# A hybrid decoder layer on one core: the MLP's first product with activations stationary, its result turned by VectorE and transfers

## The chip, the cores and the metric

The kernel runs on one core of one Trainium2 chip. Its time is the device time of one execution in microseconds (us); three executions of the kernel before took 1132.5, 1133.02 and 1133.17 us (median 1133.02). The engines are named as the profile names them: PE is TensorE's matmul, PEld its weight load, DVE is VectorE, ACT is ScalarE, POOL is GpSimd, SP is the engine that issues nearly all DMAs.

## The reference, cut to what matters

One layer on 256 tokens of width 2048, all in float32: RMSNorm, one input projection, two kinds of attention, an output projection added to the residual, then RMSNorm, an MLP and a last RMSNorm. The change is in the MLP:

```python
h = rmsnorm(x, ln2[l])                                       # 256 x 2048
x = x + jnp.square(jax.nn.relu(h @ w_mlp_in[l])) @ w_mlp_out[l]   # 2048 -> 8192 -> 2048
return rmsnorm(x, ln_f)
```

## The kernel before

**Precision.** Every float32 operand of a product is split in two parts that the matmul takes, a high one (rounded) and a low one (the rest), and a product is three passes: high x high, high x low, low x high.

**Weights.** All weights come in chunks of 1 MB (512 rows by 512 columns, on 128 partitions 4 x 512 numbers), loaded by SP into a ring of buffers (three before the MLP, six in it). A chunk is two jobs. For each job ACT writes the high part `wh` (L214) and DVE the low part `wl` (L217), each 128 x 1024. The splits lie in `spool`, four buffers of each, and in the MLP every third job's (job number modulo 3 is 2) in a late pool `mlp["split"]`, two of each (L210, L874). In the MLP a split is written five jobs before its products. When a chunk's second job is split, its buffer is given to the load of a later chunk.

**The MLP** goes through the 8192 inner columns in four quarters. A quarter is four groups of `in_group` (512 inner columns each, 8 jobs) and then four groups of `out_group` (512 output columns each, 8 jobs). `in_group` uses `products_T` (L264): the weights are stationary, and the activations move. For each 128 inner columns and each 128 rows of weights there are two matmuls: `wh` against both parts of the activations side by side, 512 moving columns (L271), and `wl` against the high part, 256 moving columns (L276). A job has 8 of each. The result stands with inner columns on partitions, which is how `out_group` needs it as its stationary operand. `out_group` uses `products_acc` (L248): activations stationary, 512 columns of weights moving, three matmuls (L258, L259, L260) for each 128 rows of weights and each 128 tokens, 12 in a job.

**After an `in_group`**, `evacuate` runs for each of its four 128-column blocks as the block's last matmul ends: ACT copies one half of the bank (L712), DVE adds the other (L714), takes relu and square in one instruction (L715), ACT rounds to the high part (L716), DVE makes the low part (L717). The results are the eight pairs `aT` of the quarter. Each `out_group` reads them in order, so the last `in_group`'s two pairs are needed from its seventh and eighth job on.

**Order.** Program order is the order in which the Python code runs: at job i the splits up to job i + 5 are asked for, then come the products, then what stands in `after`, then up to two steps of waiting side tasks (`tick`). A planner then orders each engine's instructions by a simulated timeline; on the chip every engine takes its own in that order. Accumulators of the MLP go round seven banks of PSUM.

**Where things lie.** Pools stand one behind another in each partition: `cpool`, `wpool`, `spool` (tiles of 4096 bytes), `apool` (16 tiles of 4096 bytes, all activations), `tiny` (21 tags of four buffers), and in the MLP `mlp_sb` (before: three `t1` and three `s` of 1024 bytes, and `lnf` of 8192, 14,336 bytes in all), `mlp_w` (three of 8192 bytes) and `mlp_split`.

Of the kernel before, what the change touches and what calls it, by code (L numbers as in the profile page):

```python
# [10 lines left out]
F32 = mybir.dt.float32  # L11
F32R = mybir.dt.float32r
BF16 = mybir.dt.bfloat16
AF = mybir.ActivationFunctionType
ALU = mybir.AluOpType
# [3 lines left out]
P = 128  # L19
S = 256  # L20
D = 2048
DFF = 4 * D
NT = S // P
KT = D // P
NB = 512
CK = 4
HK = 2
# [17 lines left out]
def tile_hybrid_layer(  # L45
# [21 lines left out]
    nc = tc.nc  # L67
# [5 lines left out]
    apool = ctx.enter_context(tc.tile_pool(name="apool", bufs=16))  # L73
# [91 lines left out]
    def add_chunk(view, products, after=None, pools=None):  # L165
        c = len(chunks)
        chunks.append(view)
        nh = CK // HK
        for h in range(nh):
            jobs.append((c, h, products, after if h == nh - 1 else None, pools))  # L170
# [3 lines left out]
    mlp = {"n": 0}  # L174
# [48 lines left out]
    side = deque()  # L223
    hooks = {}

    def tick(n=2):
        for task in list(side)[:n]:
            try:
                next(task)
            except StopIteration:  # L230
                side.remove(task)
# [16 lines left out]
    def products_acc(get_acc, act, k0, first, last):  # L248
        def f(h, wh, wl):
            acc = get_acc()  # L250
            for j in range(HK):
                kt = k0 + h * HK + j
                a = act(kt)
                for t in range(NT):
                    st = slice(t * P, (t + 1) * P)
                    s0 = first and h == 0 and j == 0
                    s1 = last and h == CK // HK - 1 and j == HK - 1
                    nc.tensor.matmul(acc[t], a[:, 0, st], wh[:, j, :], start=s0, stop=False)  # L258
                    nc.tensor.matmul(acc[t], a[:, 0, st], wl[:, j, :], start=False, stop=False)  # L259
                    state["mm"] = nc.tensor.matmul(acc[t], a[:, 1, st], wh[:, j, :], start=False, stop=s1)  # L260
        return f


    def products_T(get_acc, act, k0, done):  # L264
        def f(h, wh, wl):
            acc = get_acc()
            last = k0 + (h + 1) * HK == KT

            def high(i, j):
                kt = k0 + h * HK + j  # L270
                nc.tensor.matmul(acc[i], wh[:, j, i * P:(i + 1) * P], act(kt).rearrange("p a s -> p (a s)"),  # L271
                                 start=kt == 0, stop=False, skip_group_check=True)

            def low(i, j):
                kt = k0 + h * HK + j
                state["mm"] = nc.tensor.matmul(acc[i][:, S:2 * S], wl[:, j, i * P:(i + 1) * P], act(kt)[:, 0, :],  # L276
                                               start=False, stop=kt == KT - 1, skip_group_check=True)


            tiles = range(NB // P)  # L280
            for part in ([(i,) for i in tiles] if last else [tiles]):
                for one in (high, low):
                    for i in part:
                        for j in range(HK):
                            one(i, j)
                if last:
                    done(part[0])
        return f
# [393 lines left out]
    def bank(name):  # L682
        i = mlp["n"] % 7
        mlp["n"] += 1
        pool = mlp["ps"] if i < 3 else ps_acc
        return pool.tile([P, NB], F32, tag="acc", name=name)
# [3 lines left out]
    aT = {}  # L690
    ss3 = cpool.tile([P, NT, 5], F32, name="ss3")
    rs2 = {}

    def in_group(q, g):
        f0 = (q * FG + g) * NB
        acc = {}

        def get_acc():
            if not acc:
                for i in range(NB // P):  # L700
                    acc[i] = bank(f"ia{q}{g}{i}")
            return acc

        def evacuate(i):
            nm = f"{q}{g}{i}"
            kt = g * 4 + i
            if i % 2 == 0:
                pair = apool.tile([P, HK, 2, S], F32R, tag="act", name=f"aT{nm}")
                aT[q, kt // 2] = pair
            pair = aT[q, kt // 2]  # L710
            t1 = mlp["sb"].tile([P, S], F32, tag="t1", name=f"t1_{nm}")
            nc.scalar.copy(t1, acc[i][:, S:2 * S])  # L712
            s = mlp["sb"].tile([P, S], F32, tag="s", name=f"s_{nm}")
            nc.vector.tensor_tensor(s, acc[i][:, 0:S], t1, op=ALU.add)  # L714
            nc.vector.scalar_tensor_tensor(s, s, 0.0, s, op0=ALU.max, op1=ALU.mult)  # L715
            nc.scalar.copy(pair[:, i % 2, 0, :], s)  # L716
            nc.vector.tensor_tensor(pair[:, i % 2, 1, :], s, pair[:, i % 2, 0, :].bitcast(F32),  # L717
                                    op=ALU.subtract)

        for c in range(KT // CK):  # L720
            view = w_mlp_in[0, c * CK * P:(c + 1) * CK * P, f0:f0 + NB].rearrange("(k p) n -> p k n", p=P)
            add_chunk(view, products_T(get_acc, act_xs2, c * CK, evacuate))

    def out_group(q, nb):
        acc = {}

        def get_acc():
            if not acc:
                for t in range(NT):
                    acc[t] = bank(f"ma{q}{nb}{t}")  # L730
            return acc

        def act(kt):
            return aT[q, kt // 2][:, kt % 2]

        def after():
            for t in range(NT):
                residual(nb, t, acc[t], slice(0, NB))
                if q == FQ - 1:
                    square_sum(nb, t, slice(0, NB), nb)  # L740
                    nc.vector.tensor_tensor(xt[nb][:, t, :], xt[nb][:, t, :],
                                            lnf_t[:, nb * NB:(nb + 1) * NB], op=ALU.mult)

        r0 = q * (DFF // FQ)
        views = [w_mlp_out[0, r0 + c * CK * P:r0 + (c + 1) * CK * P,
                           nb * NB:(nb + 1) * NB].rearrange("(k p) n -> p k n", p=P)
                 for c in range(KT // CK)]
        if (q, nb) != (FQ - 1, 3):
            for c in range(KT // CK):
                add_chunk(views[c], products_acc(get_acc, act, c * CK, c == 0, c == KT // CK - 1),  # L750
                          after if c == KT // CK - 1 else None)
            return


        kept = {}
        half = NB // 2

        def passes(o, t, cs, kt, w):
            a = act(kt)
            wh, wl = w  # L760
            st = slice(t * P, (t + 1) * P)
            j = kt % HK
            nc.tensor.matmul(o, a[:, 0, st], wh[:, j, cs], start=kt == 0, stop=False)
            nc.tensor.matmul(o, a[:, 0, st], wl[:, j, cs], start=False, stop=False)
            nc.tensor.matmul(o, a[:, 1, st], wh[:, j, cs], start=False, stop=kt == KT - 1)

        def first_token_tile(c):
            def f(h, wh, wl):
                kept[c * (CK // HK) + h] = (wh, wl)
                for j in range(HK):  # L770
                    passes(get_acc()[0], 0, slice(0, NB), c * CK + h * HK + j, (wh, wl))
            return f

        def first_done():
            residual(nb, 0, acc[0], slice(0, NB))
            base = square_base(0, nb)
            square_sum(nb, 0, slice(0, NB), nb)
            finish_tokens(0, base)

        def second_token_tile(hc):  # L780
            def f(h, wh, wl):
                o = acc[1] if hc == 0 else bank("ma_last")
                cs = slice(hc * half, (hc + 1) * half)
                for kt in range(KT):
                    passes(o[:, :half], 1, cs, kt, kept[kt // HK])
                residual(nb, 1, o[:, :half], cs)
                if hc == 1:
                    base = square_base(1, nb + 1)
                square_sum(nb, 1, cs, nb + hc)
                if hc == 1:  # L790
                    finish_tokens(1, base)
            return f

        act_tag = (apool, "act")
        for c in range(KT // CK):
            add_chunk(views[c], first_token_tile(c), first_done if c == KT // CK - 1 else None,
                      (act_tag, act_tag) if c < 2 else None)
        for hc in range(2):
            jobs.append((None, 0, second_token_tile(hc), None, None))
# [71 lines left out]
    lnf_t = mlp["sb"].tile([P, D], F32, tag="lnf", name="lnf_t", bufs=1)  # L871
    nc.sync.dma_start(lnf_t, ln_f.partition_broadcast(P))
    mlp["w"] = ctx.enter_context(tc.tile_pool(name="mlp_w", bufs=W_BUFS))
    mlp["split"] = ctx.enter_context(tc.tile_pool(name="mlp_split", bufs=2))  # L874
    for _ in range(W_BUFS):
        issue_dma()
# [49 lines left out]
```

## Time and profile before

| | us |
|---|---|
| median of three executions | 1133.02 |
| the profiled execution's own time | 1131.97 |
| its span | 1130.3 |
| PE busy | 1119.3 (99%) |
| DVE busy | 662.8 (59%) |
| ACT busy | 536.8 (47%) |

The span runs from the first to the last instruction of the profiled execution; 1.67 us of its time lie around it. A matmul's busy time overlaps with its neighbours', since matmuls are pipelined: PE's pace is read from starts, or from the length of a stretch and its count of matmuls. The chain that ended last is PE for 99% of the span. The granted clock of PE is 1.00 of full speed in all stages of the MLP.

### The profile page before, as it was taken

What the parts mean: (1) busy time and instruction counts of PE and PEld (TensorE: products, weight loads), DVE (VectorE), ACT (ScalarE), POOL (GpSimd) and SP (SyncE); (2) the same over time, 40 slices, a digit from 0 to 9 for tenths busy, and PEclk for the clock granted to TensorE, in tenths of its full rate; (3) what the DMA queues carried; (4) which work ended last, traced back from release to release, by engine and by line L of the source; (5) the groups of instructions that cost most, each with busy time, mean ns of one, the idle gap of its engine ahead of it and who ended that gap; (6) DMA issues with size and microseconds to landing.
All of it is one profiled execution on the core that took longest, in us unless ns stands there. A gap on an engine that the chain in (4) does not pass through costs nothing.

```text
span 1130.3 us, 14306 instructions
## 1 busy us (share of the span) xinstructions
PE 1119.3 (99%) x5725; PEld 945.4 (84%) x5725; DVE 662.8 (59%) x929; ACT 536.8 (47%) x761; POOL 2.9 (0%) x16
## 2 busy tenths in 40 slices
PE   9999999999999999999999999999999999999996
PEld 6887888888888888888888888888888888888886
DVE  5756657756556565664455565455655544665752
ACT  5644545555555554543334444334544334454531
POOL 1000000000000000000000000000000000000000
PEclk9999999999999999999999999999999999999999
DMA  8745453555456855555556555555555556555502
GB/s 288 233 158 169 164 186 113 183 165 166 157 177 244 286 186 186 186 187 186 191 192 202 193 189 183 192 186 186 188 190 182 194 195 205 188 186 187 192 32 75
DMA packets 105207, 207.68 MB, mean 184 GB/s; under 512 B 4114, under 2 KB 5172, under 8 KB 105012
## 3 DMA queue, kind: packets, MB, share of 16 engines
q1 hardware_dynamic: 104852, 206.24, 55.0%
q8 instruction: 45, 0.74, 0.3%
q10 hardware_dynamic: 288, 0.52, 0.1%
q14 instruction: 22, 0.18, 0.0%
HBM read 204.65 MB, written 2.10 MB: 183 GB/s over the span
## 4 chain that ended last, share of the span: by engine, by line
PE 99%; DMA 0%; DVE 0%; SPq 0%; ACT 0%; issue 0%; DVEq 0%; ACTq 0%
PE ia L271 21%; PE ia L276 11%; PE ma L260 10%; PE ma L259 10%; PE ma L258 10%; PE acc_sk L271 3%; PE acc_sq L271 3%; PE oacc L260 3%; PE oacc L258 3%; PE oacc L259 3%; PE acc_dq L258 1%; PE acc_sq L276 1%; PE acc_sk L276 1%; PE acc_dk L258 1%; PE acc_dk L260 1%; PE acc_dq L260 1%
## 5 line engine op out<-in xcount | busy, mean ns | idle before, releaser
L217 DVE TENSOR_TENSOR wl<-w,wh 128x1024 fp32r<-128x1024 f32 (+1 forms) x385 | 469.6, 1222 | 383.7 <-ACT wh L214 382.3
L214 ACT CAST wh<-w 128x1024 fp32r<-128x1024 f32 (+1 forms) x385 | 402.0, 1047 | 465.7 <-PE ma L260 189.3
L271 PE MATMUL ia<-xs,wh 128*128 128x512 f32 x1024 | 267.7, 393 | 0.0
L271 PEld LDWEIGHTS ia<-xs,wh 128*128 128x128 f32 x1024 | 180.0, 189 | 28.4
L260 PE MATMUL ma<-wh,aT 128*128 128x512 f32 x480 | 187.9, 391 | 0.0
L259 PE MATMUL ma<-wl,aT 128*128 128x512 f32 x480 | 187.8, 391 | 0.0
L258 PE MATMUL ma<-wh,aT 128*128 128x512 f32 x480 | 187.7, 391 | 0.0
L276 PEld LDWEIGHTS ia<-xs,wl 128*128 128x128 f32 x1024 | 147.8, 189 | 15.8
L276 PE MATMUL ia<-xs,wl 128*128 128x256 f32 x1024 | 152.2, 282 | 0.0
L260 PEld LDWEIGHTS ma<-wh,aT 128*128 128x128 f32 x480 | 90.1, 188 | 19.8
L259 PEld LDWEIGHTS ma<-wl,aT 128*128 128x128 f32 x480 | 90.1, 188 | 19.8
L258 PEld LDWEIGHTS ma<-wh,aT 128*128 128x128 f32 x480 | 90.1, 188 | 19.7
L258 PE MATMUL oacc<-wh,mixT 128*128 128x512 f32 x128 | 50.6, 395 | 0.0
L259 PE MATMUL oacc<-wl,mixT 128*128 128x512 f32 x128 | 50.2, 392 | 0.0
L260 PE MATMUL oacc<-wh,mixT 128*128 128x512 f32 x128 | 49.9, 394 | 0.0
L271 PE MATMUL acc_sk<-xs,wh 128*128 128x512 f32 x128 | 36.7, 399 | 0.0
L271 PE MATMUL acc_sq<-xs,wh 128*128 128x512 f32 x128 | 34.9, 397 | 0.0
L712 ACT COPY t<-ia 128x256 f32<-128x256 f32 x64 | 23.8, 372 | 20.0 <-PE ia L276 20.0
L260 PEld LDWEIGHTS oacc<-wh,mixT 128*128 128x128 f32 x128 | 24.0, 188 | 5.0
L258 PEld LDWEIGHTS oacc<-wh,mixT 128*128 128x128 f32 x128 | 24.1, 188 | 4.9
L259 PEld LDWEIGHTS oacc<-wl,mixT 128*128 128x128 f32 x128 | 24.1, 188 | 4.9
L714 DVE TENSOR_TENSOR s<-ia,t 128x256 f32<-128x256 f32 x64 | 26.9, 420 | 1.9
(223 smaller groups left out, 1099.1 us busy)
## 6 DMA issues: line engine op xcount, KB each, us to landing
w<-in_w_mlp_in_dram SPq DMA_DIRECT2D x64, 1024.0 KB, 5.5
w<-in_w_mlp_out_dram SPq DMA_DIRECT2D x64, 1024.0 KB, 5.1
w<-in_w_in_dram SPq DMA_DIRECT2D x46, 1024.0 KB, 5.2
w<-in_w_out_dram SPq DMA_DIRECT2D x16, 1024.0 KB, 5.1
w<-in_w_in_dram SPq DMA_DIRECT2D x4, 512.0 KB, 7.9
x<-in_x_dram SPq DMA_DIRECT2D x3, 512.0 KB, 10.5
lnf_t<-in_ln_f_dram SPq DMA_DIRECT2D x1, 1024.0 KB, 6.4
out_dram<-x SPq DMA_DIRECT2D x4, 256.0 KB, 3.0
```

What stands on the lines that cost most here:

```text
L214: state["wh"] = nc.scalar.copy(wh[:, j], w[:, j])
L217: state["wl"] = nc.vector.tensor_tensor(wl[:, j], w[:, j], wh[:, j].bitcast(F32), op=ALU.subtract)
L258: nc.tensor.matmul(acc[t], a[:, 0, st], wh[:, j, :], start=s0, stop=False)
L259: nc.tensor.matmul(acc[t], a[:, 0, st], wl[:, j, :], start=False, stop=False)
L260: state["mm"] = nc.tensor.matmul(acc[t], a[:, 1, st], wh[:, j, :], start=False, stop=s1)
L271: nc.tensor.matmul(acc[i], wh[:, j, i * P:(i + 1) * P], act(kt).rearrange("p a s -> p (a s)"), start=kt == 0, stop=False, skip_group_check ...
L276: state["mm"] = nc.tensor.matmul(acc[i][:, S:2 * S], wl[:, j, i * P:(i + 1) * P], act(kt)[:, 0, :], start=False, stop=kt == KT - 1, skip_g ...
L712: nc.scalar.copy(t1, acc[i][:, S:2 * S])
L714: nc.vector.tensor_tensor(s, acc[i][:, 0:S], t1, op=ALU.add)
```

## The change

`in_group` now uses `products_acc` as `out_group` does: activations stationary, weights moving, two accumulators of 128 tokens x 512 inner columns. Its result has tokens on partitions. A side task turns it: DVE transposes blocks of 32 x 32 out of PSUM into `bl`, 16 DMAs issued by SP move the blocks between partitions into `hT`, DVE takes relu and square of `hT` in one instruction of 128 x 1024, and ACT and DVE write two pairs `aT` of 128 x 512 per part. `mlp_sb` then holds `hT` and `bl` (4096 bytes each) and `lnf`, 16,384 bytes. A tile of 352 numbers (1408 bytes) is put ahead of `mlp_split`.

```diff
+        def turn_task():
+            hT = mlp["sb"].tile([P, NT * 4, 4, 32], F32, tag="hT", name=f"hT{q}{g}", bufs=1)
+            bl = mlp["sb"].tile([P, NT, 4, 4 * 32], F32, tag="bl", name=f"bl{q}{g}", bufs=1)
+            for t in range(NT):
+                nc.vector.transpose(bl[:, t].rearrange("p f (k b) -> p f k b", b=32),
+                                    acc[t].rearrange("p (k f a) -> p f k a", k=4, f=4))
+            hv = hT.rearrange("p (t i) k b -> p t i (k b)", t=NT)
+            for i in range(4):
+                for f in range(4):
+                    nc.sync.dma_start(hv[f * 32:(f + 1) * 32, :, i, :], bl[i * 32:(i + 1) * 32, :, f, :])
+            yield
+            nc.vector.scalar_tensor_tensor(hT, hT, 0.0, hT, op0=ALU.max, op1=ALU.mult)
+            for kk in range(2):
+                pair = apool.tile([P, HK, 2, S], F32R, tag="act", name=f"aT{q}{g}{kk}")
+                s = hT[:, :, kk * 2:kk * 2 + 2, :].rearrange("p i k b -> p k i b")
+                hi = pair[:, :, 0, :].rearrange("p k (i b) -> p k i b", b=32)
+                lo = pair[:, :, 1, :].rearrange("p k (i b) -> p k i b", b=32)
+                nc.scalar.copy(hi, s)
+                nc.vector.tensor_tensor(lo, s, hi.bitcast(F32), op=ALU.subtract)
+                aT[q, g * 2 + kk] = pair
+                yield
+
+        def after():
+            side.append(turn_task())
+            tick(1)
...
-            add_chunk(view, products_T(get_acc, act_xs2, c * CK, evacuate))
+            add_chunk(view, products_acc(get_acc, act_xs2, c * CK, c == 0, c == KT // CK - 1),
+                      after if c == KT // CK - 1 else None)
...
         def act(kt):
+            while (q, kt // 2) not in aT:
+                tick()
             return aT[q, kt // 2][:, kt % 2]
...
     mlp["w"] = ctx.enter_context(tc.tile_pool(name="mlp_w", bufs=W_BUFS))
+    gap = ctx.enter_context(tc.tile_pool(name="mlp_gap", bufs=1))
+    gap.tile([P, 352], F32, name="mlp_gap")
     mlp["split"] = ctx.enter_context(tc.tile_pool(name="mlp_split", bufs=2))
```

## Rows read from the trace of the kernel before

**Rows 1.** The page: busy time, and the chain that ended last

```profile
PE 1119.3 (99%) x5725; PEld 945.4 (84%) x5725; DVE 662.8 (59%) x929; ACT 536.8 (47%) x761; POOL 2.9 (0%) x16
...
PE 99%; DMA 0%; DVE 0%; SPq 0%; ACT 0%; issue 0%; DVEq 0%; ACTq 0%
```

**Rows 2.** Windows of MLP stages, in_groups and out_groups in turn

```profile
core 0: us, PE busy (x) PEld busy (x) DVE busy (x) ACT busy (x) POOL busy (x), PEclk, DMA share, GB/s
410.00:500.38 90.38, 90.38 (x521) 79.21 (x520) 55.91 (x81) 45.25 (x68) 0.00 (x0) 1.00 0.59 191
500.38:588.37 87.99, 87.99 (x386) 72.09 (x385) 46.52 (x48) 35.15 (x37) 0.00 (x0) 1.00 0.56 187
588.37:677.92 89.55, 89.55 (x514) 78.56 (x512) 53.84 (x74) 42.58 (x60) 0.00 (x0) 1.00 0.58 193
677.92:765.92 88.00, 88.00 (x387) 72.10 (x385) 46.53 (x48) 35.13 (x37) 0.00 (x0) 1.00 0.57 187
765.92:855.45 89.53, 89.53 (x513) 78.56 (x512) 53.89 (x74) 42.58 (x60) 0.00 (x0) 1.00 0.58 193
855.45:943.39 87.94, 87.94 (x386) 72.09 (x385) 46.47 (x48) 35.14 (x37) 0.00 (x0) 1.00 0.57 186
943.39:1033.01 89.62, 89.62 (x514) 78.57 (x512) 53.90 (x74) 42.57 (x60) 0.00 (x0) 1.00 0.59 193
```

**Rows 3.** PE timeline: first matmuls of five successive out_group jobs (start, length)

```profile
500.38 0.40 PE L258 MATMUL ma<-wh,aT 128*128 128x512 f32 x1
...
503.11 0.40 PE L258 MATMUL ma<-wh,aT 128*128 128x512 f32 x1
...
505.90 0.39 PE L258 MATMUL ma<-wh,aT 128*128 128x512 f32 x1
...
508.64 0.39 PE L258 MATMUL ma<-wh,aT 128*128 128x512 f32 x1
...
511.36 0.40 PE L258 MATMUL ma<-wh,aT 128*128 128x512 f32 x1
```

**Rows 4.** Groups by form (count | busy us, mean ns | idle us): DVE, ACT

```profile
L217 DVE TENSOR_TENSOR wl<-w,wh 128x1024 fp32r<-128x1024 f32 x383 | 468.3, 1225 | 383.7 <-ACT wh L214 382.3
L714 DVE TENSOR_TENSOR s<-ia,t 128x256 f32<-128x256 f32 x64 | 26.9, 420 | 1.9
L428 DVE COPY T_dk<-tp_dk 128x512 f32<-128x512 f32 x4 | 2.8, 692 | 1.4 <-PE tp_dk L425 1.4
L847 DVE TENSOR_SCALAR x<-x,rf 128x512 f32<-128x512 f32 x2 | 1.0, 482 | 0.0
L716 ACT CAST aT<-s 128x256 fp32r<-128x256 f32 x64 | 24.2, 404 | 0.5
L156 ACT ACTIVATE mixT<-mtp_d,ghd 128x512 fp32r<-128x512 f32 x4 | 2.8, 688 | 3.7 <-PE mtp_d L446 3.7
```

**Rows 5.** SP timeline: four stores in a row; then the stores' time to landing

```profile
1113.74 1.88 SPq L848 DMA_DIRECT2D out_dram<-x  x4
...
DMA to landing us min/median/max: 1.9/2.5/3.0
```

**Rows 6.** SP timeline: weight loads about the second in_group's end, and that end on PE

```profile
455.33 0.40 PE L276 MATMUL ia<-xs,wl 128*128 128x256 f32 x2
...
451.62 0.37 SPq L195 DMA_DIRECT2D w<-in_w_mlp_in_dram  x1
457.87 0.37 SPq L195 DMA_DIRECT2D w<-in_w_mlp_out_dram  x1
...
w<-in_w_mlp_in_dram SPq DMA_DIRECT2D x64, 1024.0 KB, 5.5
```

**Rows 7.** Waits: who waited for whom, total us, times, longest

```profile
ACT wh L214 <- PE ma L260: 189.3, 116, 4.5
...
SPq L195 <- DVE wl L217: 772.3, 151, 13.3
```

**Rows 8.** DVE timeline after the first in_group: a split among the evacuation's instructions

```profile
433.88 0.43 DVE L715 SCALAR_TENSOR_TENSOR s<-s 128x256 f32<-128x256 f32 x1
434.26 1.23 DVE L217 TENSOR_TENSOR wl<-w,wh 128x1024 fp32r<-128x1024 f32 x1
435.40 1.09 DVE L717 TENSOR_TENSOR aT<-s,aT 128x256 fp32r<-128x256 f32 x3
```

**Rows 9.** SP timeline: small loads at the kernel's start, behind large ones

```profile
9.58 0.32 SPq L87 DMA_DIRECT2D rows<-in_diff_head_norm_dram  x1
...
18.45 0.33 SPq L91 DMA_DIRECT2D lamv<-in_lambda_k_dram  x1
```

More of the change, by code (lines that the diff above doesn't have):

```diff
@@ L699, in get_acc @@
             if not acc:
-                for i in range(NB // P):
-                    acc[i] = bank(f"ia{q}{g}{i}")
-            return acc
[L704 to L718, printed above, removed]
+                for t in range(NT):
+                    acc[t] = bank(f"ia{q}{g}{t}")
@@ new lines, in get_acc @@
+            return acc
+        def turn_task():
+            hT = mlp["sb"].tile([P, NT * 4, 4, 32], F32, tag="hT", name=f"hT{q}{g}", bufs=1)
+            bl = mlp["sb"].tile([P, NT, 4, 4 * 32], F32, tag="bl", name=f"bl{q}{g}", bufs=1)
+            for t in range(NT):
+                nc.vector.transpose(bl[:, t].rearrange("p f (k b) -> p f k b", b=32),
[15 more added lines that the diff above has]
+                yield
```

## The prediction, made before the change was run

> **What bounds the kernel now.** I read the page's busy times and its chain of waits first: PE is busy for 99% of the span and holds 99% of the chain that ended last [rows 1]. So only what changes PE's pace, or makes PE wait, can change the time. The windows by stage come next, because the page's mean hides the pace: in every MLP stage PE is busy for the whole window at a granted clock of 1.00, while DVE has 54 us of 90 and ACT 43 us [rows 2]. So the number to look for is PE's time per stage. An in_group stage (256 pairs of a 512- and a 256-column matmul) takes 89.55, 89.53 and 89.62 us, an out_group stage (384 matmuls of 512 columns) 87.99, 88.00 and 87.94 us [rows 2]. Last I read starts on PE's timeline, job by job (below).
>
> **The products (gain).** Before, an in_group stage streams 256 x (512 + 256) = 196,608 columns; after, 4 groups x 8 jobs x 12 matmuls = 384 of 512 columns, also 196,608. The columns are the same, the matmuls fewer (512 to 384). Two pairs of before are replaced by three matmuls: 2 x 89.57 / 256 = 0.6998 us against 3 x 87.98 / 384 = 0.6873 us. The new stage is instruction for instruction an out_group stage (same helper, same shapes, same operands' pools), so I take it at 87.98 us. Gain 89.57 - 87.98 = 1.59 us a stage; the first one (90.38 us, with transposes of the activations in it) gains the same 1.6. Four stages: **-6.3 us**. Bounds: nothing, if what costs time is the columns alone, and -9 if the matmuls run as in the fast jobs below, which the next edit has in its term.
>
> The Trainium skill (TensorE: Matmul & The Clock Gate, section Back-to-back issue gap) gives an isolated matmul N / 2.4 + 2.5 ns. By it two pairs would be 650 ns and three long ones 647.5, a gain of 2.5 ns x 512 such units = 1.3 us, an estimate by that page, which speaks against most of this term. The trace shows 0.6998 against 0.6873 us, so a matmul here costs more beside its columns than the page allows, and the row decides.
>
> **The bytes of the split pool (gain).** PE's starts of five successive jobs are 500.38, 503.11, 505.90, 508.64 and 511.36 us: 2.73, 2.79, 2.74, 2.72 us [rows 3]. The second of them is job 161, and 161 modulo 3 is 2: its splits lie in the late pool. The same step stands at every third job of the out_groups. That pool differs from `spool` in place alone. With 32 bytes for each of `tiny`'s 84 small buffers (an assumption), it lies 65,536 + 2688 + 14,336 + 24,576 bytes plus `spool`'s own 32,768 behind `spool`'s start, which modulo 4096 is 640. After the change it is 2688 + 16,384 + 24,576 + 1408 = 45,056 = 11 x 4096 behind `apool`, so 0 modulo 4096, like every tile of `spool` and `apool`. That the sum closes supports the assumption; that the byte modulo 4096 causes the 0.06 us is my reading of two pools, no more. In the changed kernel all MLP jobs move their splits past PE, 256 of them, a third in the late pool: 85 x 0.06 = **-5.1 us**. Bounds: nothing (the byte is not the cause) to -8.
>
> **The evacuation (taken at nothing, for it lies beside PE).** Removed in each group: on DVE 12 instructions of 0.42 us (5.0 us), on ACT four of 0.40 and four copies of about the same (3.1) [rows 4]. Added on DVE: two 32 x 32 transposes of 128 x 512 out of PSUM, which the trace of before does not show. Their bounds are 0.48 (one input, from SBUF) and 1.4 each (twice a copy out of PSUM); I take the copy out of PSUM of the same size, 0.69, as the nearest row. Then one 128 x 1024 instruction at 1.22 and two of 128 x 512 at about 0.69: 4.0 us in all; on ACT two casts of 0.69, 1.4 us [rows 4]. Both engines lose work, and both had slack. Should all of it be bare it would be some 4 us a group.
>
> **The transfers on SP.** 16 DMAs of 32 KB a group. Four stores issued in a row took 1.88 us, 0.47 each, and landed 1.9 to 3.0 us after issue [rows 5]. The trace of before has no transfer within SBUF; I take these for both prices. Issue 16 x 0.47 = 7.5 us, the last landing 2.5 us later. As upper bound stand the small loads at the start, behind large ones: seven issues from 9.58 to 18.45, 1.48 apart, so 24 us for 16 [rows 9]. What they are queued with: SP issued weight loads 4.1 us before and 2.1 us after the second group's end (455.73), and a load lands in 5.5 [rows 6], so the first is in by about 1.4 us after the end, when the transposes are done. The second and the third load now wait behind the 16 issues, up to about 8 us. That is hidden: SP mostly waits for a buffer to be split (772 us in 151 waits [rows 7]), six buffers let a load start 6 x 2 x 2.74 = 33 us before its split, and 33 - 5.5 = 27 us are to spare.
>
> **The added wait on DVE and ACT.** From the group's end: transposes 1.4, issues to 8.9, landing to 11.4, relu and square to 12.6, first cast 13.3, first low part 14.0, second pair 14.7. The quarter's last two pairs are read by the out_group from its seventh and eighth job on, 6 x 2.74 = 16.4 and 19.2 us after the end: 2.4 and 4.5 us to spare. Behind the waiting DVE instruction stand the splits. ACT waits for PE to free split buffers (189.3 us [rows 7]), so five jobs are split at the group's end, and the sixth, whose buffers come free just then, is needed 5 x 2.74 = 13.7 us later. If the planner puts this split ahead of the instruction that waits for landing, nothing is late; before, it did put splits among the evacuation's instructions [rows 8]. I take nothing. If it puts it behind the whole task, the split ends at 14.7 + 1.2 = 15.9, and PE waits 2.2 us a group.
>
> **Sum.** 1131.97 (the profiled execution's own time: span 1130.3 and 1.67 around it) - 6.3 - 5.1 = 1120.6. The median of the runs shown is 1.05 above that execution: **1121.6 us**, 1.0% faster.
>
> **Rivals.**
> 1. The byte does nothing. For it: two pools are thin evidence, and the modulus is assumed. Against: the step recurs every third job, and four buffers at different multiples of 4096 in `spool` show none. Then only the products gain: 1133.0 - 6.3 = 1126.7.
> 2. The last group's pairs come late. The margin is 2.4 us by prices that no row of before shows; splits queued between (1.05 on ACT, 1.2 on DVE) eat it, and a landing 2 us slower makes PE wait about 2 us in each quarter: 1121.6 + 4 x 2 = 1129.6. Against: the second pair has 4.5, and the splits are six jobs ahead.
> 3. It ends slower: the waiting instruction holds the splits in every group. Place: DVE's queue behind relu and square of `hT`. Price 16 x 2.2 = 35 us, so 1121.6 + 35 = 1157. It decides against the change from 11.4 / 16 = 0.7 us of PE wait a group. For it: in program order the waiting instruction stands straight behind the DMAs with no split between. Against: rows 8. Each further us to landing adds up to 16, and at the 1.48 us pitch the chain would be 16 us longer, some 18 us a group or over 1400 in all, to which I give little.
>    The Trainium skill (SBUF — State Buffer, section The DMA setup-cost knee) says each DMA pays about 2 us that does not scale with bytes, mostly completion. The 1.9 to 3.0 us to landing agree. Paid one after another they would be 32 us for 16 in a group of 22, an estimate by that page that would make SP the bound; but four stores went out in 1.88 us, so here such times overlap.
>
> **How the numbers follow.** Forecast 0.50, rival 1 0.17, rival 2 0.14, rival 3 0.19. Within 0.2% (2.3 us) is about what a measurement of this kernel can tell from no change. The forecast and the first two rivals are all faster by more than that; of rival 3 a mild form (0.6 to 0.8 us a group) lands within it, the rest is slower: faster 0.79, same 0.05, slower 0.16. The likeliest case's own range is 1118 (both terms at their larger bounds, 6.3 + 8 = 14.3 under 1133.0, rounded down) to 1125; taking in rivals 1 and 2 and the mild form of 3, the range is 1117 to 1133.
>
> **What would show it.** Right: in_group stages of about 87 us with 384 matmuls each, and every third job as long as the others (2.73). Byte wrong: every third job still 2.79, in both kinds of stage. Rival 2: PE idle before the seventh job of each quarter's first out_group, released by `aT`. Rival 3: PE idle some 14 us after each in_group's end, released by `wl`, with DVE's long idle put down to a DMA of `hT`. The prediction would be wrong as a whole if transfers within SBUF land later than about 5 us, or a transpose out of PSUM takes several us.

## The result, and the profile after

The changed kernel takes 1118.7 us (median of four, 1118.62 to 1118.77) against 1132.88 before: a ratio of 0.9875, 95% interval 0.986 to 0.9889. The forecast was 1121.6 us, a gain of 11.4 us; the gain is 14.2. The profiled execution took 1118.63 us, with a span of 1116.9.

The page after: PE still holds the span and the chain (compare [rows 1]); it has 512 matmuls fewer, and DVE and ACT have a little less to do.

```profile
PE 1106.0 (99%) x5213; PEld 919.6 (82%) x5213; DVE 652.8 (58%) x817; ACT 512.4 (46%) x665; POOL 2.9 (0%) x16
...
PE 99%; DMA 0%; DVE 0%; SPq 0%; ACT 0%; issue 0%; DVEq 0%; ACTq 0%
```

The windows of the first four MLP stages after, in_groups and out_groups in turn, columns as in [rows 2]:

```profile
409.80:497.81 88.01, 88.01 (x393) 72.81 (x392) 53.21 (x57) 39.78 (x46) 0.00 (x0) 1.00 0.61 206
497.81:584.85 87.04, 87.04 (x385) 72.07 (x384) 46.82 (x44) 34.70 (x34) 0.00 (x0) 1.00 0.61 202
584.85:671.89 87.04, 87.04 (x385) 72.07 (x384) 51.13 (x50) 36.88 (x38) 0.00 (x0) 1.00 0.62 208
671.89:758.93 87.04, 87.04 (x385) 72.07 (x384) 46.87 (x44) 34.81 (x34) 0.00 (x0) 1.00 0.62 203
```

An in_group stage and an out_group stage now take the same 87.04 us, to the hundredth. Against [rows 2] that is 2.5 us less for each in_group stage (2.4 for the first) and 0.95 us less for each out_group stage: four times 2.5 and nearly four times 0.95 are 13.6 us, all of the gain but for noise. Nothing was lost at a group's end.

PE's timeline at the first matmuls of the five jobs that [rows 3] shows of before:

```profile
497.81 0.39 PE L258 MATMUL ma<-wh,aT 128*128 128x512 f32 x1
...
500.53 0.39 PE L258 MATMUL ma<-wh,aT 128*128 128x512 f32 x1
...
503.25 0.39 PE L258 MATMUL ma<-wh,aT 128*128 128x512 f32 x1
...
505.97 0.39 PE L258 MATMUL ma<-wh,aT 128*128 128x512 f32 x1
...
508.69 0.39 PE L258 MATMUL ma<-wh,aT 128*128 128x512 f32 x1
```

Each job takes 2.72 us, also the second, whose splits lie in the late pool. Before, the jobs took 2.73, 2.79, 2.74 and 2.72.

The new instructions, by form (count | busy us, mean ns | idle us before them):

```profile
L711 DVE STREAM_TRANSPOSE bl<-ia 128x512 f32<-128x512 f32 x32 | 20.9, 692 | 0.0
L725 DVE TENSOR_TENSOR aT<-hT,aT 128x512 fp32r<-128x512 f32 x32 | 20.6, 685 | 0.0
L718 DVE SCALAR_TENSOR_TENSOR hT<-hT 128x1024 f32<-128x1024 f32 x16 | 19.5, 1222 | 2.2 <-DMA hT<-bl 1.9 <-issue 0.2
L724 ACT CAST aT<-hT 128x512 fp32r<-128x512 f32 x32 | 18.2, 617 | 1.2 <-DVE hT L718 1.1
```

The transpose costs what the copy out of PSUM did (692 ns; [rows 4]). The instruction that waits for the 16 transfers held DVE idle for 1.9 us in all 16 groups together, because the planner put the splits ahead of it.

The end of the second quarter's in_groups (671.89 us), on the timelines of DVE, SP, ACT and PE (weight loads):

```profile
671.65 1.31 DVE L711 STREAM_TRANSPOSE bl<-ia 128x512 f32<-128x512 f32 x2
...
672.98 11.19 SPq L716 DMA_DIRECT2D hT<-bl  x16
...
685.49 1.23 DVE L718 SCALAR_TENSOR_TENSOR hT<-hT 128x1024 f32<-128x1024 f32 x1 [0.21 <-DMA hT<-bl]
686.78 1.23 DVE L217 TENSOR_TENSOR wl<-w,wh 128x1024 fp32r<-128x1024 f32 x1
687.92 1.29 DVE L725 TENSOR_TENSOR aT<-hT,aT 128x512 fp32r<-128x512 f32 x2
...
686.75 1.14 ACT L724 CAST aT<-hT 128x512 fp32r<-128x512 f32 x2
...
688.44 0.19 PEld L260 LDWEIGHTS ma<-wh,aT 128*128 128x128 f32 x1
...
691.16 0.19 PEld L260 LDWEIGHTS ma<-wh,aT 128*128 128x128 f32 x1
...
697.21 1.40 DVE L819 SCALAR_TENSOR_TENSOR x<-ma,rr,x 128x512 f32<-128x512 f32 x2
715.12 1.40 DVE L819 SCALAR_TENSOR_TENSOR x<-ma,rr,x 128x512 f32<-128x512 f32 x2
736.88 1.40 DVE L819 SCALAR_TENSOR_TENSOR x<-ma,rr,x 128x512 f32<-128x512 f32 x2
758.64 1.41 DVE L819 SCALAR_TENSOR_TENSOR x<-ma,rr,x 128x512 f32<-128x512 f32 x2
```

The 16 issues took 11.2 us (0.64 apart, with one longer wait), not 7.5. The two low parts were done 1.29 us after 687.92, the first at about half of that, 688.6, 16.7 us after the group's end where 14.0 was forecast. In program order the out_group's seventh job starts 6 x 2.72 = 16.3 us after that end, and the weight load of its first low part would be the one at 688.44, before that low part was done.

PE didn't take that order. L819 adds each finished out_group to `x`: it comes 25.3 us after the stage's start for the first out_group, 17.9 later for the second, then each 21.8; in the kernel before it came 21.7 us after the start, then each 22.0. So the planner had put part of the second out_group ahead of the end of the first. The trace shows where: three matmuls of a stage wait on PE's own semaphore, each the fourth of an out_group. In the kernel before they lie 22.0 us apart (678.62, 700.63, 722.65); here they are at 672.57, 688.89 and 716.09. The second out_group therefore starts at 688.21, after six jobs of the first. The next weight load that can be the seventh job's first low part is that at 691.16, so at least 2.5 us were to spare. It is hidden, but by an order that the forecast had not assumed.

### The profile page after: what moved, and what is told of

Its sections match the earlier page's. It is cut to its first block, busy times and chain, and to the rows that moved or that the text cites. A ratio compares the mean times of both kernels' runs of the same rounds, so it can differ in the third digit from the quotient of the medians.

```text
span 1116.9 us, 13378 instructions
## 1 busy us (share of the span) xinstructions
PE 1106.0 (99%) x5213; PEld 919.6 (82%) x5213; DVE 652.8 (58%) x817; ACT 512.4 (46%) x665; POOL 2.9 (0%) x16
## 4 chain that ended last, share of the span: by engine, by line
PE 99%; DMA 0%; DVE 0%; SPq 0%; ACT 0%; issue 0%; DVEq 0%; ACTq 0%
PE ia L260 10%; PE ia L259 10%; PE ia L258 10%; PE ma L258 10%; PE ma L259 10%; PE ma L260 10%; PE acc_sk L271 3%; PE acc_sq L271 3%; PE oacc L260 3%; PE oacc L258 3%; PE oacc L259 3%; PE acc_dq L258 1%; PE acc_sq L276 1%; PE acc_sk L276 1%; PE acc_dk L258 1%; PE acc_dq L260 1%
## 5 line engine op out<-in xcount | busy, mean ns | idle before, releaser
L258 PE MATMUL ia<-wh,xs 128*128 128x512 f32 x512 | 199.4, 389 | 0.0
L260 PE MATMUL ia<-wh,xs 128*128 128x512 f32 x512 | 199.3, 389 | 0.0
L259 PE MATMUL ia<-wl,xs 128*128 128x512 f32 x512 | 199.2, 389 | 0.0
L258 PEld LDWEIGHTS ia<-wh,xs 128*128 128x128 f32 x512 | 96.1, 188 | 20.0
L259 PEld LDWEIGHTS ia<-wl,xs 128*128 128x128 f32 x512 | 96.1, 188 | 19.9
L260 PEld LDWEIGHTS ia<-wh,xs 128*128 128x128 f32 x512 | 96.1, 188 | 19.9
```

## Experiments

Two terms made the forecast, the product order and the byte of the late pool, and a third statement set the transfers at nothing. The rival for the byte was that something else in the change made the long jobs go away; for the transfers, that they are late. A run given without a ratio was executed once; what is read from it rests on the length of its stages.

**The byte, taken away and alone**

`a1_no_gap`, the changed kernel without the gap:

```diff
-    gap = ctx.enter_context(tc.tile_pool(name="mlp_gap", bufs=1))
-    gap.tile([P, 352], F32, name="mlp_gap")
```

> The changed kernel without the tile ahead of the late split pool, so the pool lies 1408 bytes lower (2688 modulo 4096 behind spool). If the pool's byte is the cause of the long jobs: every third MLP job 233 ns a matmul again and the one behind it 228, all eight stages near 88.0 us instead of 87.04, 1118.7 + 7 = about 1126 us. If something else in the change removed the long jobs (the new product order, the new tiles of mlp_sb): stages stay at 87.04 and the time at 1118.7.

Measured: 1126.66 us (0.9941 of before, 0.9925 to 0.9958). Windows of an in_group and an out_group stage:

```profile
586.78:674.70 87.92, 87.92 (x385) 72.08 (x384) 51.09 (x50) 36.82 (x38) 0.00 (x0) 1.00 0.61 208
674.70:762.72 88.02, 88.02 (x385) 72.08 (x384) 46.80 (x44) 34.63 (x34) 0.00 (x0) 1.00 0.60 199
```

Both stages are back at 88.0. By the ratios, each against runs of before on the same chip, the rest of the change is worth 0.0059 x 1133 = 6.7 us and the gap 0.0066 x 1133 = 7.5; by the stages, 4 x 1.6 = 6.4 and 8 x 0.94 = 7.5.

`a2_byte_alone`, the kernel before with the pool moved to the same byte:

```diff
+    gap = ctx.enter_context(tc.tile_pool(name="mlp_gap", bufs=1))
+    gap.tile([P, 864], F32, name="mlp_gap")
     mlp["split"] = ctx.enter_context(tc.tile_pool(name="mlp_split", bufs=2))
```

> The kernel before with one edit: a tile of 864 numbers (3456 bytes) ahead of the late split pool, which moves it from 640 to 0 modulo 4096. If the byte is the cause: out_group stages fall from 88.0 to 87.04 us, in_group stages (weights stationary there, no long jobs seen) stay at 89.5, so 1132.9 - 3.7 = about 1129 us. If it is not: 1132.9.

Measured: 1129.24 us (0.9963 of before, 0.9948 to 0.9978). Its windows, an in_group and an out_group stage:

```profile
588.90:678.29 89.39, 89.39 (x513) 78.55 (x512) 53.90 (x74) 42.57 (x60) 0.00 (x0) 1.00 0.60 193
678.29:765.36 87.07, 87.07 (x387) 72.08 (x385) 46.44 (x48) 35.23 (x37) 0.00 (x0) 1.00 0.57 188
```

The out_group stage falls by 0.9 us, the in_group stage hardly moves, and the time falls by 0.0037 x 1133 = 4.2 us. So the two edits don't add up one by one (4.2 and 6.7 against 14.2): once in_group moves the splits past PE too, the byte counts in all eight stages.

**Which byte counts, and against what**

Three runs changed only the size of the gap (`[P, 352]` to 224, 336 and 288), two moved whole pools.

```diff
-    gap.tile([P, 352], F32, name="mlp_gap")
+    gap.tile([P, 224], F32, name="mlp_gap")   # a3; 336 in a4, 288 in c3
```

> The changed kernel with 224 numbers in the gap instead of 352: the late pool lies 512 bytes lower than spool's byte modulo 4096. If the address counts modulo 512 or less: 87.04 us a stage and 1118.7. If it counts modulo 1024 or more: long jobs again, up to 1126.

Measured: 1118.38 us, stages of 87.04 us.

> The changed kernel with 336 numbers in the gap instead of 352: the late pool lies 64 bytes lower than spool's byte. If the address counts modulo 64 or less: 1118.7. If 64 bytes off are enough to disturb: long jobs, up to 1126; in between if the disturbance grows with the distance.

Measured: 1127.74 us. An in_group and an out_group stage:

```profile
587.97:676.03 88.06, 88.06 (x386) 72.00 (x384) 51.11 (x50) 36.83 (x38) 0.00 (x0) 1.00 0.62 207
676.03:764.17 88.14, 88.14 (x386) 71.99 (x384) 46.80 (x44) 34.63 (x34) 0.00 (x0) 1.00 0.60 199
```

> The changed kernel with 288 numbers in the gap: the late pool lies 256 bytes lower. If 256 bytes are the period: 1118.7 us. If 512: long jobs at every third, 1126 to 1128 us.

Measured: 1118.78 us, stages of 87.04 us. So 256 and 512 bytes off are free, and 64 bytes cost a little more than the 128 modulo 256 of the kernel before (640) and of the run without a gap (2688).

`c1_stationary_64`:

```diff
+    shift = ctx.enter_context(tc.tile_pool(name="shift", bufs=1)); shift.tile([P, 16], F32, name="shift_t")
     apool = ctx.enter_context(tc.tile_pool(name="apool", bufs=16))
...
-    gap.tile([P, 352], F32, name="mlp_gap")
+    gap.tile([P, 336], F32, name="mlp_gap")
```

> The changed kernel with 64 bytes put between spool and apool and 64 taken from the gap: every moving operand (the splits, in both pools) stays at its byte, every stationary one (the activations) lies 64 bytes further. If the distance between moving and stationary operand modulo 512 decides: every products_acc job is long now, about 233 ns a matmul, some 4200 matmuls x 6.6 ns = 28 us more, about 1146 us. If the moving operand's own address decides: 226.7 ns and 1118.7 us.

Measured: 1144.58 us, near the 1146 of the first theory. In the MLP no address that PE streams had moved. An in_group and an out_group stage:

```profile
596.27:685.87 89.60, 89.60 (x385) 71.91 (x384) 51.27 (x50) 36.64 (x38) 0.00 (x0) 1.00 0.61 205
685.87:775.47 89.60, 89.60 (x385) 71.89 (x384) 46.80 (x44) 34.58 (x34) 0.00 (x0) 1.00 0.59 194
```

All jobs are long now: 89.60 / 384 is 233.3 ns a matmul against 226.7.

`c2_all_64`, the 64 bytes ahead of the weights' pools as well:

```diff
+    shift = ctx.enter_context(tc.tile_pool(name="shift", bufs=1)); shift.tile([P, 16], F32, name="shift_t")
     wpool = ctx.enter_context(tc.tile_pool(name="wpool", bufs=W_BUFS))
...
-    gap.tile([P, 352], F32, name="mlp_gap")
+    gap.tile([P, 224], F32, name="mlp_gap")
```

> The changed kernel with 64 bytes put ahead of all pools of weights and activations, and the late pool 512 bytes back (224 numbers in the gap, which the run with that gap alone showed to cost nothing): all distances between operands as in the changed kernel modulo 512, all addresses 64 bytes further. If distances decide: 1118.7 us. If addresses decide: the jobs change, up to 1146 us.

Measured: 1119.08 us:

```profile
585.38:672.42 87.04, 87.04 (x386) 72.12 (x384) 51.21 (x50) 36.86 (x38) 0.00 (x0) 1.00 0.62 209
```

It is the distance between the moving and the stationary operand that decides, not the address of either: at the multiples of 256 bytes that were tried a matmul takes 226.7 ns, at the distances tried in between (64 bytes off, and 128 modulo 256) about 233.

**What the products gained from**

`e1_cut_pass`, the same columns in as many matmuls as before:

```diff
+                    if cut:
+                        nc.tensor.matmul(acc[t][:, :S], a[:, 1, st], wh[:, j, :S], start=False, stop=s1, ...)
+                        state["mm"] = nc.tensor.matmul(acc[t][:, S:], a[:, 1, st], wh[:, j, S:], start=False, stop=s1, ...)
+                        continue
                     state["mm"] = nc.tensor.matmul(acc[t], a[:, 1, st], wh[:, j, :], start=False, stop=s1)
```

> The changed kernel with one of the three passes of in_group (low x high, L260) cut into two matmuls of 256 columns: columns as before, 128 matmuls more in each in_group stage, 512 in a stage as in the kernel before. If a matmul costs about 13 ns beside its columns (226.7 - 213.3 at 512 columns, 120 - 106.7 at 256, both from traces here): 4 x 128 x 13.3 ns = 6.8 us more, 1125.5 us. If the kernel before also paid for changing between lengths (9.4 us in all at the good byte): up to 1128. If columns alone count: 1118.7; by the Trainium skill's 2.5 ns a matmul: 1120.0.

Measured: 1126.78 us. An in_group and an out_group stage:

```profile
586.66:675.83 89.17, 89.17 (x514) 77.81 (x513) 51.33 (x50) 36.77 (x38) 0.00 (x0) 1.00 0.60 201
675.83:762.88 87.05, 87.05 (x387) 72.07 (x386) 46.75 (x44) 34.70 (x34) 0.00 (x0) 1.00 0.62 205
```

128 matmuls more cost 89.17 - 87.04 = 2.1 us a stage, 16.6 ns each, and bring the stage near the 89.39 us of the old order at the good byte. Columns alone, and 2.5 ns a matmul, are ruled out. But the cut adds changes of length along with the count, so 16.6 ns is not the price of a matmul alone. PE's starts tell the two apart:

```profile
601.28 0.40 PE L258 MATMUL ia<-wh,xs 128*128 128x512 f32 x1
601.51 0.40 PE L259 MATMUL ia<-wl,xs 128*128 128x512 f32 x1
601.75 0.28 PE L261 MATMUL ia<-wh,xs 128*128 128x256 f32 x1
601.87 0.27 PE L263 MATMUL ia<-wh,xs 128*128 128x256 f32 x1
601.98 0.40 PE L258 MATMUL ia<-wh,xs 128*128 128x512 f32 x1
```

Next to short matmuls the long ones take 231 to 236 ns instead of 226.7, and the short ones 113 to 119 instead of the 120 that they take one behind another in the kernel before. At steady lengths, two short ones for a long one cost 240 - 226.7 = 13.3 ns, 1.7 us for 128. So about 1.7 of the 2.35 us that the order gained at the good byte (89.39 - 87.04) is the count of matmuls; the other 0.6 goes with the changes of length, which the old order had too (8 long and 8 short in a job).

**The transfers: left out, doubled, and spread**

`d2_no_transfers` leaves out the movement between partitions:

```diff
-                nc.vector.transpose(bl[:, t]..., acc[t]...)
...
-                    nc.sync.dma_start(hv[f * 32:(f + 1) * 32, :, i, :], bl[i * 32:(i + 1) * 32, :, f, :])
+                nc.vector.transpose(hw[:, t], acc[t].rearrange("p (k f a) -> p f k a", k=4, f=4))
```

> The changed kernel without the 16 transfers of each group: VectorE's transposes write the tile that relu and square read, so the blocks of 32 x 32 stay in the partitions they came from (a part of the computation left out). If the transfers are hidden altogether, as PE's stages of 87.04 us say: 1118.7 us, stages unchanged. If they cost PE something that its stages don't show (shared memory, late weights): less than 1118.4.

Measured: 1119.48 us, stages of 87.04 us as with them; the 0.8 us more lie ahead of the MLP, whose first matmul started at 411.06 us instead of 409.80. The transfers cost PE nothing that these stages show.

`d1_double_dmas`:

```diff
-                    nc.sync.dma_start(hv[f * 32:(f + 1) * 32, :, i, :], bl[i * 32:(i + 1) * 32, :, f, :])
+                    for t in range(NT):
+                        nc.sync.dma_start(hv[f * 32:(f + 1) * 32, t, i, :], bl[i * 32:(i + 1) * 32, t, f, :])
```

> The changed kernel with each of the 16 transfers within SBUF cut in two (32 a group, half the bytes each). SP issues one each 0.64 us, so the chain from a group's end to its pairs grows by some 10 us. If the last group of each quarter has no more margin than the trace of the changed kernel shows (its first low part ended 0.05 us before the matmul that reads it): PE waits about 10 us in each quarter, 1118.7 + 40 = about 1159 us, idle before the seventh and eighth job of the quarter's first out_group. If the transfers have room: 1118.7. If DVE's queue holds the splits: PE waits in all 16 groups, 1118.7 + 100 and more.

Measured: 1206.5 us, twice the loss expected. An in_group and an out_group stage:

```profile
607.89:694.93 87.04, 87.04 (x385) 72.07 (x384) 48.07 (x46) 35.65 (x36) 0.00 (x0) 1.00 0.50 167
694.93:803.93 109.00, 92.05 (x385) 75.04 (x384) 49.52 (x48) 35.92 (x36) 0.00 (x0) 0.91 0.58 195
```

All of it is in the out_group stages, some 22 us each: in this one PE is idle for 17.0 us, waiting mostly for ACT's cast of `aT` and that for the transfers, and busy for 5.0 us longer at a lower granted clock. The in_group stages keep 87.04, so the splits were not held up there. From the waits of PE and of SP's queue (us in total, times, longest), then SP's timeline:

```profile
PE ma L258 <- ACT aT L725: 53.2, 8, 9.3
...
SPq L717 <- DMA w<-in_w_mlp_out_dram: 56.4, 28, 2.6
...
630.10 20.52 SPq L717 DMA_DIRECT2D hT<-bl  x32
...
658.62 25.74 SPq L717 DMA_DIRECT2D hT<-bl  x32
...
690.44 26.19 SPq L717 DMA_DIRECT2D hT<-bl  x32
...
722.80 27.00 SPq L717 DMA_DIRECT2D hT<-bl  x32
```

The stage is the one that the second rival names, and the sign too (PE waits for `aT`), but the loss is of another kind. 32 issues keep SP for 20.5 to 27.0 us, where a group's products take 21.8, so each group's transfers start later behind its end than those of the group before: 0.5, 7.2, 17.3 and 27.9 us in this quarter. PE waits twice a quarter (8 waits in all), for the third group's pairs and for the fourth's. Into the issues goes SP's waiting for weight loads to land, about 14 us a quarter. I had counted 10 us once a quarter and neither the delay that adds up from group to group nor the clock. The premise, 0.05 us of margin, was a misreading (see the profile after), so this run shows what too many transfers cost, not how little margin the 16 had.

`d3_double_two_queues`, the same 32 with every second one issued by ACT:

```diff
-                        nc.sync.dma_start(hv[f * 32:(f + 1) * 32, t, i, :], ...)
+                        (nc.sync if t == 0 else nc.scalar).dma_start(hv[f * 32:(f + 1) * 32, t, i, :], ...)
```

> The kernel with 32 half transfers a group, every second one issued by ACT instead of SP. If issue time on SP's queue was what made the 32 late (16 x 0.64 us more, and SP standing behind weight loads): each queue has 16 again, 1118.7 us, or a little more where ACT issues late. If the number of transfers or their landing made them late: near 1206 again.

Measured: 1176.08 us, so neither theory's number. From its waits:

```profile
ACT wh L214 <- DMA hT<-bl: 210.1, 16, 15.6
```

Now ACT's splits stand behind ACT's waits for transfers, once in each of the 16 groups, and PE waits in both kinds of stage (the two of the second quarter take 91.66 and 95.43 us): the third rival, on ACT instead of DVE. Since a second change (ACT's queue) came in with the spreading, this run doesn't tell whether issue time alone made the 32 late.

**The same edit elsewhere**

`f1_turn_sqsk` uses the product order and the turning for the four projections that still had weights stationary:

```diff
-            add_chunk(view, products_T(get_acc, act_xs, c * CK, done), after if c == KT // CK - 1 else None)
+            add_chunk(view, products_acc(get_acc, act_xs, c * CK, c == 0, c == KT // CK - 1),
+                      after if c == KT // CK - 1 else None)
```

> The changed kernel with its product order and its turning used for the four projections of the stick-breaking queries and keys too (activations stationary, VectorE transposes, 16 transfers each, then the row factor). Products: four groups of 22.4 us at 21.76, so -2.5 us: 1116.2 us, if nothing waits. If the keys of the last head group, now some 18 us later, hold up the attention before the output projection: PE waits there and the time is 1118.7 or more.

Measured: 1120.32 us (0.9883 of before, 0.9867 to 0.99), no better than the changed kernel. Its MLP starts at 412.33 us instead of 409.80, and its waits show PE held up once for the attention's result:

```profile
PEld oacc L258 <- ACT mixT L156: 1.5, 1, 1.5
```

The changed kernel has no such wait. That is part of where the expected 2.5 us went; the rest was not traced.

## Why the prediction was right, point by point

- **What bounds the kernel.** Right: PE's pace was the only thing that moved, and PE's windows account for 13.6 of 14.2 us.
- **The products, -6.3 us.** Right, at the bad byte: 6.4 us by the stages, 6.7 by the ratio, between the kernel before and the run without the gap, with stages of 88.0 as taken from the out_groups. The reason given, a cost of each matmul beside its columns, holds for most of it: 13.3 ns for each one added, at steady lengths; the rest goes with changes of length, which I had not named. The 2.5 ns that the Trainium skill gives for an isolated matmul (TensorE: Matmul & The Clock Gate, section Back-to-back issue gap), by which `e1_cut_pass` would have been 1120.0 us, do not hold in this stream: it was 1126.78.
- **The byte, -5.1 us.** The mechanism was right and the term mis-sized: it measured 7.5 us, and that is where the 2.8 us between forecast and result lie, nearly all of them. I compared the long job (2.79) with the mean of the others (2.73). One of those is the job behind it, long itself (2.74 against 2.72 after). Against the 2.72 of the undisturbed job the same rows give 0.07 and 0.02 more, 85 x 0.09 = 7.7. The stage after tells the same: 0.95 us for 32 jobs, 8 x 0.95 = 7.6. I had read the cause as the address modulo 4096; multiples of 256 are free and 128 is slow, and what counts is the distance to the stationary operand, which I had not put forward.
- **The evacuation, nothing.** Right; the transposes took 692 ns where 690 were taken.
- **The transfers, nothing.** Right in the time, wrong in the price: 0.64 us to issue one where 0.47 was taken from the stores [rows 5], while 1.9 us to landing lay at the low end. The chain to the first low part took 16.7 us instead of 14.0, which in the order that I had assumed would have used up the whole margin of 2.4 us and some 0.2 us more. That it cost nothing is luck as far as the forecast goes: the planner had put a job of the second out_group in between. The weight loads wait behind the issues, and PE did not wait for them.
- **The added wait on DVE.** Right: the planner put the splits ahead, as in [rows 8].
- **Rivals.** The first fell with `a1_no_gap` and `a2_byte_alone`. The second did not happen, by the planner's order and not by the margin given; `d1_double_dmas` shows its wait, with other causes in its size. The third is real once the splits share a queue with the transfers (`d3_double_two_queues`). The chances do not quite follow from the cases: the likeliest case and the first two rivals, all called faster, have 0.81, and 0.79 was put down for faster.

## What to carry to other kernels

Where PE never waits, compare the length of stages that stream the same columns in different ways: the difference of 1.6 us between two kinds of stage held the whole of the first term. Look for jobs of equal work that take unequal time, compare them with an undisturbed one and over a whole stage, and ask where in memory each one's operands lie. A chain that is hidden may have any margin: before adding to it, look at what reads its end, in the order that the engine took and not in program order.

## What the runs showed of the hardware that was not expected

- With float32 operands of 512 moving columns, a matmul took 226.7 ns when the moving and the stationary operand lay a multiple of 256 bytes apart in the partition, and about 233 ns at 64 or 128 bytes off it (1118.7 against 1144.6 us when all jobs were 64 off). The Trainium skill (TensorE: Matmul & The Clock Gate, section Step-by-step: what each phase is for) says that loading the next weights takes no read bandwidth from the running matmul. No run here measures that by itself; what the runs do show is a matmul's time that depends on where its stationary operands lie, by 6.6 ns. That the two reads collide in memory is an inference.
- In a stream of matmuls of one length a step was 226.7 ns at 512 columns and 120 at 256; where lengths change it was 231 to 236 for the long ones and 113 to 119 for the short.
- A transfer of 32 KB between partitions took 0.64 us of SP's time to issue and 1.9 us (median) to land.
- After the waits of the doubled transfers PE's granted clock was 0.91 as a mean of the out_group stage, 1.00 in the stages where it never waited. Right behind the wait that ended at 719.95 us it was 0.50, the 1.2 GHz level, and matmuls of 512 columns started 427 ns apart.
